# One transformer layer on one core: squares ahead of the last x tile, a held load, a third bank for A0b, the gate's row sum in two fp32r parts, and seventeen steps moved by a few matmuls

## The chip, the cores and the metric

The kernel runs on one core of a Trainium2 chip. The metric is device time in microseconds of that core. Five engines have queues of their own: PE (matmuls), ACT and DVE (elementwise work), POOL (slower elementwise work, and some DMAs) and SP (DMAs). They meet only at semaphores.

## The reference

One layer over 512 tokens of width 1024, in fp32:

```python
hn = rms_norm(h, ln_mix); z = hn @ w_in          # q1 q2 k1 k2 va | qf kf vf fg | qc kc vc
... per-head rms_norm of q and k, times a gain
o_a = diff_attention(...)        # 4 heads: softmax(q1 k1) - lam * softmax(q2 k2), then a per-head norm
o_b = forgetting_attention(...)  # 6 heads, bias from the cumulative sum of log_sigmoid(fg)
o_c = chunk_attention(...)       # 6 heads
h = h + concat(o_a, o_b, o_c) @ w_out
h = h + conv_gated_mlp(rms_norm(h, ln_ffn), w_up, conv_w, conv_b, w_down)
h = h + (p @ w_ple_proj) * sigmoid(rms_norm(h, ln_ple) @ w_ple_gate)
```

## The kernel before

**Precision.** A product of two fp32 matrices is three fp32r matmuls: each factor is split into a rounded part (`_h`, an ACT cast) and the rest (`_l`, a DVE subtraction); high by high, low by high and high by low are accumulated in one PSUM bank. `Th`, `Tl` are the split activations, feature by token; `A_0_h`, `A1b_l`, `w_hi`, `w_lo` and the like are split weights. `A_0_r`, `A1b_r`, `w_raw` are the raw weights as they land.

**Units and slots.** The input projection has eight column groups: A0 and A1 (two halves of the heads of group A), B0 to B2, C0 to C2. A0 and A1 each have a second part, A0b and A1b, with their second queries and keys. Each group is done in four units, one for each 128 tokens t, of 24 matmuls. A unit is a slot: `first_products` is slots 0 to 3 (A0), A0b is 4 to 7, A1 8 to 11, A1b 12 to 15, B0 16 to 19, and so on; the output projection follows from slot 40. In the trace A0 and A1 read alike (`A_z`, `A_zn`), and so do heads.

**After a unit** its bank `z` is evacuated: ACT squares the query and key columns (`A0b_sq`), DVE sums them by head (`A0b_rs`, a reduce, then a tensor_scalar, called TS below), POOL raises the result to the power -1/2 (also `A0b_rs`), DVE multiplies (`A0b_zn`). When all four t are done, `feature_cols` transposes `zn` on PE into a bank (`A_q_p`, then `A_k_p`; four transposes each), ACT and DVE split them (`A_q_q`, `A_q_ql`, `A_k_k`, `kl`) and POOL moves halves (`A_q_q`, `A_k_k` on POOL). Then come scores (`A_s`, `A_0b_s` and `A_1b_s`: part b is the second softmax), softmax pieces on DVE and ACT (`A_e`, `A_st`), transposes of the probabilities (`A_pt`, `A_ptc`, split into `pth`, `ptl`, `ptc`) and products with V (`A_po`). For group B, `forget_cumsum` transposes the gate columns (`pf`), scans them on DVE (`fs`) and transposes the sums back (`pq`).

**Banks.** PSUM has eight: z (2), s (2), t (3) and o (1). `in_unit` gives the four A0b units a bank by the letters of `"tots"[t]`: t, o, t, s. The first products hold both z and both s banks, `z0`.

**Order.** PE's order is written by hand: `run` takes one projection matmul after the other (index j, 0 to 23 in a slot) and puts in the next piece of an attention step at (slot, j) of the table `T`, with at least 3 matmuls between two pieces. The other engines' orders are made by a scheduler that follows data and a priority, raised for steps in `EARLY`. The numbers `wA1b`, `wO6` and the like in `T` say how many of a weight's four low parts POOL makes instead of DVE (by DMA that accumulates, or by a subtraction). The MLP and the gate are ordered by a planner, `Task` by `Task`, from costs and engine lists.

**The gate at the end.** Eight column blocks of h are squared on ACT (`n_sq`), added up on POOL or DVE (`sums`), and `total` sums over the partitions with one fp32 matmul by a matrix of ones (`pst<-sums,onec`). From `pst` come the row scales; the gate products `pg` do not wait for them, the outputs `y` do.

Of the kernel before, what the change touches and what calls it, by code (L numbers as in the profile page):

```python
# [15 lines left out]
P = 128  # L16
D = 1024
S = 512
# [59 lines left out]
def kernel(ctx: ExitStack, tc: tile.TileContext, x, xt0, xt, pt_in, small, bias_c,  # L78
# [53 lines left out]
    dve.memset(nhalf, -0.5)  # L132
    onec = cp.tile([P, 1], F32, tag="onec", name="onec")
    dve.memset(onec, 1.0)
    epsc = cp.tile([P, 1], F32, tag="epsc", name="epsc")
    dve.memset(epsc, EPS)
    ident = cp.tile([P, P], F32, tag="ident", name="ident")
# [153 lines left out]
    def load_x(t):  # L291
        tc.keep_in_program_order(nc.sync.dma_start(out=h[:, t, :], in_=x[t * P : (t + 1) * P, :]))
# [21 lines left out]
    for b in range(2):  # L314
        for i in range(2):
            c = HALF[1 - i]
            tc.keep_in_program_order(nc.gpsimd.tensor_scalar(
                KL[b][i][c, :], onec[c, :].broadcast_to([HD, S]), 0.0, 1.0, ALU.mult, ALU.mult))

    DONE = set()  # L320
# [14 lines left out]
    def first_products():  # L335
        for k in range(KD):
            n = 3 * P + 6
            if k % 2 == 0:
                wh, wl = (pi.tile([P, 768 + ROOM], F32R, tag=f"w{q}", bufs=W[q], name=f"A0_{k // 2}_{q}") for q in ("hi", "lo"))
            a = slice((k % 2) * n, (k % 2 + 1) * n)  # L340
            th, tl = Th[k // 4][:, k % 4, :], Tl[k // 4][:, k % 4, :]
            g = h[:, 3, 0:1] if k == 0 else col(C_MIX, k)
            if k == 0:
                for c in (slice(0, H), slice(H, S)):
                    dve.tensor_scalar(th[:, c], XB[k][:, c], g, 1.0, ALU.mult, ALU.mult)
            elif k == 3:
                dve.tensor_scalar(th, XB[k], g, 1.0, ALU.mult, ALU.mult)
            else:
                act.activation(th, XB[k], AF.Copy, scale=g)
            act.copy(wh[:, a], WA[k])  # L350
            dve.tensor_tensor(out=wl[:, a], in0=WA[k], in1=f32(wh[:, a]), op=ALU.subtract)
            dve.scalar_tensor_tensor(tl, XB[k], g, f32(th), ALU.mult, ALU.subtract)
            for i, (ta, w) in enumerate(((Th, wh), (Th, wl), (Tl, wh))):
                for t in range(NT):
                    pe.matmul(z0[t][:, :n], tcol(ta, k, t), w[:, a], start=k == 0 and i == 0, stop=k == KD - 1 and i == 2)
            if k == 1:
                load_x(3)
        ws = [w() for w in first_b]
        for t in range(NT):
            stats(t)  # L360
        ev = [in_unit("A0", 0, 3 * P + 6, t, None, []) for t in range(NT)]

        rs = [ev[t][0](rest=False) for t in range(2)]
        for t in range(NT):
            ev[t][1](rs[t])
            if t < 2:
                rs.append(ev[t + 2][0](rest=False))
        for t in range(NT):
            ev[t][0](sums=False)
        return ws  # L370
# [54 lines left out]
                                       rs[:, 4:8].unsqueeze(2).broadcast_to([P, 4, HD]), ALU.mult, ALU.mult)  # L425

    def feature_cols(zn, j, name):
        pt = bank("t", f"{name}_p")
        for t in range(NT):
            pe.transpose(pt[:, t * P : (t + 1) * P], zn[:, t, j * P : (j + 1) * P], ident)  # L430
        return pt
# [92 lines left out]
    def forget_cumsum():  # L524
# [199 lines left out]
    pairs = ["A0", "A1", "B0", "B1", "B2", "C0", "C1", "C2"]  # L724
    steps = {}

    def at(slot, gen, *args, start=1, early=0):
        steps.setdefault(slot, []).append((start, early, gen, args))

    def step(early, g):  # L730
        if early:
# [4 lines left out]

    def run(fill, todo):

        todo = [(start, early, gen(*args)) for start, early, gen, args in todo]
        after = 0  # L740
        for j in range(3 * KD):
            next(fill, None)
            while todo and j >= max(todo[0][0], after):
                try:
                    step(*todo[0][1:])
                    after = j + 3
# [5 lines left out]
        for _, early, g in todo:  # L752
# [6 lines left out]
    T = {  # L759
# [13 lines left out]
    }  # L773
    EARLY = {
# [6 lines left out]
    }  # L781

    def add(key, gen, *args):
        at(T[key][0], gen, *args, start=T[key][1], early=EARLY.get(key, 0))

    def lo_by(key, n):

# [3 lines left out]
    add("A0a", qk_cols, "A0", 0)  # L791
    add("A0b", qk_cols, "A0", 1)
    add("fc", forget_cumsum)
    add("A1a", qk_cols, "A1", 0)
    add("A1b", qk_cols, "A1", 1)
    for pr in ("A0", "A1"):
# [69 lines left out]
    slot = 0  # L866
    slot = 4
    act.pinned = dve.pinned = True
    ws_b = first_products()
    act.pinned = dve.pinned = False  # L870
    first_done = act.last, dve.last
    lam_init()
    def load_next(f, nxt, j):
        if j > 1:
            nxt.append(f())
# [51 lines left out]
    def mtmp(dt, m, name):  # L927
        return mp.tile([P, S * m], dt, tag="conv", bufs=CONV, name=name)
# [3 lines left out]
    def square(j):  # L932
        sq = mtmp(F32, 1, f"sq{j}")
        act.activation(sq, hj(j), AF.Square)
        return sq

    def total(tag, sums):

        pst = bank(tag, "pst")
        pe.matmul(pst, onec.broadcast_to([P, P]), sums, start=True, stop=True)  # L940
        return pst

    def roots(pst, rb, mt, sq):
# [468 lines left out]

    def first_load():
        q = loads.pop(0)
        q.do()
        q.end = 0.0

    def first_split(f, i, later=False):
# [215 lines left out]
        square3(j)  # L1634
    pst_slot, root_slots = Slot("t"), [Slot("conv"), Slot("conv")]

    def sums3():
# [200 lines left out]
```

## Time and profile before

| what | value |
|---|---|
| median of 3 runs | 689.13 us (688.67 to 690.82) |
| profiled execution: time, span | 689.12 us, 687.2 us |
| instructions | 12200 |
| busy PE, DVE, ACT, POOL | 98%, 81%, 61%, 33% of the span |
| mean granted PE clock | 0.998 |
| moved by DMA | 134.63 MB, mean 196 GB/s |

The page's share of busy time is over the whole span. The attention part reaches to about 303 us, the MLP to about 638, the gate to the end.

### The profile page before, as it was taken

The page shows a single profiled execution, that of the slowest core. Times are in us where ns is not written, and L with a number is a line of the kernel's source. Part 1 is how long each engine was busy: PE and PEld are TensorE (multiplying, and loading weights), DVE is VectorE, ACT ScalarE, POOL GpSimd, SP SyncE. Part 2 cuts the span into 40 slices and gives each one's busy share as a digit, 9 for nine tenths or more (in the row PEclk, how much of TensorE's full clock was granted, in tenths as well). Part 3 has the DMA queues.
Part 4 walks back from the last instruction along what each step waited for, and adds up shares of the span by engine and source line. Part 5 has one row for each costly group of instructions (what it writes and reads, how often), then busy time and mean ns, then how long its engine had stood idle before and what let it go on. Part 6 is the DMA issues. An engine that isn't in the chain of part 4 may idle for free.

```text
span 687.2 us, 12200 instructions
## 1 busy us (share of the span) xinstructions
PE 676.3 (98%) x4244; PEld 618.7 (90%) x4244; DVE 558.3 (81%) x1166; ACT 417.8 (61%) x811; POOL 227.9 (33%) x340
## 2 busy tenths in 40 slices
PE   9999999999999999999999999999999999999997
PEld 8988989998999988878889899999998898999886
DVE  7677787988878875789888897799888889888863
ACT  7657876776757653565576645556554566556821
POOL 6576765766564530421212111212111200000210
PEclk9999999999999999999999999999999999999999
DMA  9565679856655264389999899999999985462441
GB/s 329 200 169 115 193 239 275 235 172 213 228 136 186 87 220 139 122 203 244 164 271 219 170 263 234 268 219 203 223 287 259 176 217 155 145 229 95 153 123 61
DMA packets 57400, 134.63 MB, mean 196 GB/s; under 512 B 6486, under 2 KB 8150, under 8 KB 57340
## 3 DMA queue, kind: packets, MB, share of 16 engines
q1 hardware_dynamic: 45660, 107.60, 47.6%
q0 software_dynamic: 11392, 25.96, 23.1%
q8 instruction: 33, 0.54, 0.3%
q10 hardware_dynamic: 288, 0.31, 0.1%
q14 instruction: 27, 0.22, 0.1%
HBM read 125.83 MB, written 44.05 MB: 247 GB/s over the span
## 4 chain that ended last, share of the span: by engine, by line
PE 86%; DVE 4%; DMA 4%; ACT 2%; POOL 2%; issue 1%; SPq 0%; ACTq 0%; POOLq 0%; DVEq 0%
PE u L104 22%; PE dn_X L104 9%; PE C_z L104 6%; PE pg L104 6%; PE wo L104 6%; PE B_z L104 5%; PE sX L104 5%; PE dn_Y L104 4%; PE sY L104 3%; PE sZ L104 3%; PE dn_Z L104 2%; PE A1b_z L104 2%; PE pp L104 2%; DMA h<-in_x_dram 1%; PE B_s L104 1%; PE C_s L104 1%
## 5 line engine op out<-in xcount | busy, mean ns | idle before, releaser
L104 DVE TENSOR_TENSOR w_lo<-w_raw,w_hi 128x768 fp32r<-128x768 f32 (+5 forms) x154 | 115.0, 787 | 9.0 <-ACT w_hi L104 8.8
L104 ACT CAST w_hi<-w_raw 128x768 fp32r<-128x768 f32 (+5 forms) x154 | 99.6, 688 | 36.6 <-PE dn_X L104 7.1
L104 PE MATMUL u<-Th,w_hi 128*128 128x512 f32 x224 | 87.0, 391 | 0.0
L104 PE MATMUL u<-Tl,w_hi 128*128 128x512 f32 x224 | 86.9, 390 | 0.0
L104 PE MATMUL u<-Th,w_lo 128*128 128x512 f32 x224 | 86.8, 390 | 0.0
L104 PEld LDWEIGHTS u<-Th,w_lo 128*128 128x128 f32 x224 | 42.1, 188 | 9.0
L104 PEld LDWEIGHTS u<-Th,w_hi 128*128 128x128 f32 x224 | 42.0, 188 | 8.6 <-ACT Th L104 0.4
L104 PEld LDWEIGHTS u<-Tl,w_hi 128*128 128x128 f32 x224 | 42.1, 188 | 8.0
L104 DVE SCALAR_TENSOR_TENSOR c<-u,cols,c 128x511 f32<-128x511 f32 (+1 forms) x56 | 41.0, 746 | 6.2 <-ACT c L104 5.7
L104 POOL DMA_DIRECT2D usum<-usum x16 | 13.0, 812 | 91.5 <-DMA usum<-in_w_up_dram 56.9
L104 PE MATMUL dn_X<-g_ah,w_hi 128*128 128x256 f32 x144 | 39.8, 276 | 0.0
L104 PE MATMUL dn_X<-g_ah,w_lo 128*128 128x256 f32 x144 | 39.8, 276 | 0.0
L104 PE MATMUL dn_X<-g_al,w_hi 128*128 128x256 f32 x144 | 39.8, 276 | 0.0
L104 PE MATMUL B_z<-B_h,Th 128*128 128x384 f32 x96 | 33.5, 349 | 0.2 <-DVE A_st L104 0.2
L104 PE MATMUL C_z<-C_h,Th 128*128 128x384 f32 x96 | 33.5, 349 | 0.0
L104 PE MATMUL B_z<-B_l,Th 128*128 128x384 f32 x96 | 32.8, 342 | 0.0
L104 PE MATMUL B_z<-B_h,Tl 128*128 128x384 f32 x96 | 32.8, 342 | 0.0
L104 PE MATMUL C_z<-C_h,Tl 128*128 128x384 f32 x96 | 32.7, 341 | 0.0
L104 PE MATMUL C_z<-C_l,Th 128*128 128x384 f32 x96 | 32.5, 339 | 0.0
L104 ACT ACTIVATE c<-u,cols 128x512 f32<-128x512 f32 x28 | 21.5, 775 | 16.0 <-PE u L104 14.6
L104 POOL DMA_DIRECT2D dsum<-dsum x16 | 13.0, 813 | 51.8 <-DMA dsum<-dsum 22.2
L104 POOL TENSOR_TENSOR sums<-sums,n_sq 128x512 f32<-128x512 f32 x3 | 3.9, 1291 | 78.7 <-ACT n_sq L104 78.6
(501 smaller groups left out, 2381.5 us busy)
## 6 DMA issues: line engine op xcount, KB each, us to landing
w_raw<-in_w_up_dram SPq DMA_DIRECT2D x44, 384.0 KB, 7.0
dsum<-in_w_dsum_dram SPq DMA_DIRECT2D x12, 768.0 KB, 8.5
w_raw<-dsum SPq DMA_DIRECT2D x24, 384.0 KB, 5.9
usum<-in_w_usum_dram SPq DMA_DIRECT2D x32, 256.0 KB, 5.9
w_raw<-in_w_down_dram SPq DMA_DIRECT2D x18, 384.0 KB, 6.0
w_raw<-usum SPq DMA_DIRECT2D x16, 384.0 KB, 7.1
B_r<-in_w_in_dram SPq DMA_DIRECT2D x12, 384.0 KB, 3.8
C_r<-in_w_in_dram SPq DMA_DIRECT2D x12, 384.0 KB, 5.2
```

The lines of the kernel that those rows point to most:

```text
L104: ins = getattr(self.eng, op)(*a, **k)
```

## The change

It has seven parts.

1. **First products.** The square sum of the last x tile, `stats(3)`, stands behind the squares of the first two A0 units on ACT. `lam_init` is held behind a DVE instruction of k = 4. Two of the four `kl` fills go from POOL to DVE, and a ones column `oner` in fp32r is made on DVE.
2. **Banks.** A0b's unit t = 3 takes a t bank in place of an s bank; the transposes of A0's first queries and keys take s banks in place of t banks.
3. **`forget_cumsum` is cut in two.** The transposes back (`pq`) are a step of their own, `fq`, at (12, 0).
4. **`T`, `EARLY`, gaps.** Seventeen steps start one to ten matmuls earlier or later (`A0b` eight later, `A0n` ten later). `A1s12` has pieces 2 matmuls apart. The evacuations of seven units get a priority of their own, `A0b` gets 80, `A0n` and `A1b` lose theirs.
5. **Low parts.** A1b's fourth low part is a DVE subtraction and no longer an ACT copy and an accumulating POOL DMA; one more low part of the output weights is made on POOL.
6. **A held load.** The `w_up` load of 384 KB that SP issued at 14.57 us is issued behind SP's last instruction at that place of the program, among the loads near 280 us.
7. **The gate's sum.** `sums` is split into `sums_h` (an ACT cast) and `sums_l` (a DVE subtraction), and two fp32r matmuls take the place of the fp32 one. The planner's list has a task more there and orders some squares, splits and adds anew.

```diff
     def first_products():
...
+            if k == 4:
+                mid.append(dve.last)
...
-        for t in range(NT):
+        for t in range(3):
             stats(t)
         ev = [in_unit("A0", 0, 3 * P + 6, t, None, []) for t in range(NT)]
 
         rs = [ev[t][0](rest=False) for t in range(2)]
+        for t in range(3, NT):
+            stats(t)
...
-        pt = bank("t", f"{name}_p")
+        pt = bank("s" if name in ("A0_q0", "A0_k0") else "t", f"{name}_p")
...
-        evac()
+        with ahead(f"e{slot}"):
+            evac()
...
-            z = bank("tots"[t] if pr == "A0" else "z", f"{name}_z{t}")
+            z = bank("tott"[t] if pr == "A0" else "z", f"{name}_z{t}")
...
+        X["fs"] = fs
         yield
+
+    def forget_cols():
+        fs = X["fs"]
         pq = bank("t", "pq")
...
-        "A0a": (7, 8), "A0b": (9, 13), "fc": (11, 5), ...
+        "A0a": (7, 9), "A0b": (9, 21), "fc": (11, 3), ...
...
-        "wA1a": (0, 0), "wA1b": (1, 0), ... "wO6": (0, 1),
+        "wA1a": (0, 0), "wA1b": (0, 0), ... "wO6": (0, 2), "fq": (12, 0),
...
+    def two_parts(sums):
+
+        hi, lo = (mtmp(F32R, 1, f"sums_{q}") for q in "hl")
+        act.copy(hi, sums)
+        dve.tensor_tensor(out=lo, in0=sums, in1=f32(hi), op=ALU.subtract)
+        return hi, lo
...
+    def total_of_parts(tag, hi, lo):
+
+        pst = bank(tag, "pst")
+        pe.matmul(pst, oner.broadcast_to([P, P]), hi, start=True, stop=False)
+        pe.matmul(pst, oner.broadcast_to([P, P]), lo, start=False, stop=True)
         return pst
...
     def first_load():
         q = loads.pop(0)
-        q.do()
+        with tc.issue_after(sp.last):
+            q.do()
...
     def sums3():
-        v3["pst"] = total("t", v3["sums"])
+        v3["pst"] = total_of_parts("t", *v3["parts"])
...
     def at_sums():
-        p = pe_task(8, sums3, (), [v3["last"]], [pst_slot], [sum_slot])
+        slots = [Slot("conv"), Slot("conv")]
+        a = Task("do", [AC(S), DV(S)], parts3, [v3["last"]], slots, [sum_slot])
+        p = pe_task(4, sums3, (), [a], [pst_slot], slots)
```

PE's order around A0b's query and key transposes, first before and then changed (`A_z_625` and `A_z_627` are the same unit of A1, `A_z_693` the next):

```order
L104 MATMUL A_z_625<-A_2_l,Th_65 128x384
L104 MATMUL A_q_p<-ident,A0b_zn 128x128 x4
L104 MATMUL A_z_625<-A_2_h,Tl_67 128x384
L104 MATMUL A_z_625<-A_2_h,Th_65 128x384
L104 MATMUL A_z_625<-A_2_l,Th_65 128x384
L104 MATMUL A_k_p<-ident,A0b_zn 128x128 x4
```

```order
L104 MATMUL A_z_627<-A_3_h,Th_65 128x384
L104 MATMUL A_q_p<-ident,A0b_zn 128x128 x4
L104 MATMUL A_z_627<-A_3_l,Th_65 128x384
L104 MATMUL A_z_627<-A_3_h,Tl_67 128x384
L104 MATMUL A_k_p<-ident,A0b_zn 128x128 x4
L104 MATMUL A_z_693<-A_0_h,Th_64 128x384
```

Eight projection matmuls that stood behind the first group of transposes stand ahead of it; the scores that come later keep their place.

DVE's order from the low parts of A1b to A0b's last `zn`, before and changed (the tiles `A0b_rs_572` and `A0b_rs_574` are those of t = 3):

```order
L104 TENSOR_REDUCE A0b_rs_572<-A0b_sq_570 128x4
L104 TENSOR_TENSOR A1b_l<-A1b_r,A1b_h 128x512 x3
L104 TENSOR_SCALAR A0b_rs_572<-A0b_rs_572,rstd 128x4
L104 SCALAR_TENSOR_TENSOR A_V<-A_z_585,rstd,A_V 128x128
L104 TENSOR_REDUCE A_rs_614<-A_sq_612 128x4
L104 SCALAR_TENSOR_TENSOR A0b_zn<-A0b_z_519,A0b_rs_572 128x256
```

```order
L104 TENSOR_TENSOR A1b_l<-A1b_r,A1b_h 128x512
L104 TENSOR_SCALAR A0b_rs_510<-A0b_rs_510,rstd 128x4
L104 TENSOR_TENSOR A1b_l<-A1b_r,A1b_h 128x512
L104 TENSOR_REDUCE A0b_rs_574<-A0b_sq_572 128x4
L104 TENSOR_TENSOR A1b_l<-A1b_r,A1b_h 128x512 x2
L104 SCALAR_TENSOR_TENSOR A_V<-A_z_587,rstd,A_V 128x128
L104 TENSOR_SCALAR A0b_rs_574<-A0b_rs_574,rstd 128x4
L104 SCALAR_TENSOR_TENSOR A0b_zn<-A0b_z_483,A0b_rs_510 128x256
L104 TENSOR_REDUCE A_rs_616<-A_sq_614 128x4
L104 SCALAR_TENSOR_TENSOR A0b_zn<-A0b_z_521,A0b_rs_574 128x256
```

There are four subtractions in place of three ahead of the TS of t = 3, the TS of t = 2 is there too, and A_V comes ahead of the last TS.

DVE's order at the gate's sum, changed (before, the four adds were followed at once by the `wg_al` rows):

```order
L104 SCALAR_TENSOR_TENSOR xl<-w_raw_3897,cols,xh 128x512
L104 TENSOR_TENSOR sums_7364<-sums_7364,n_sq_7591 128x512
L104 TENSOR_TENSOR sums_7364<-sums_7364,n_sq_7630 128x512
L104 TENSOR_TENSOR sums_7364<-sums_7364,n_sq_7633 128x512
L104 TENSOR_TENSOR sums_7364<-sums_7364,n_sq_7636 128x512
L104 TENSOR_TENSOR sums_l<-sums_7364,sums_h 128x512
L104 SCALAR_TENSOR_TENSOR wg_al<-w_raw_3899,cols,wg_ah 128x512
```

A subtraction that waits for ACT's cast of the finished sum has come in between.

More of the change, by code (lines that the diff above doesn't have):

```diff
@@ L134 @@
     dve.memset(onec, 1.0)
+    oner = cp.tile([P, 1], F32R, tag="oner", name="oner")
+    dve.tensor_scalar(oner, onec, 1.0, 1.0, ALU.mult, ALU.mult)
     epsc = cp.tile([P, 1], F32, tag="epsc", name="epsc")
@@ L316 @@
             c = HALF[1 - i]
-            tc.keep_in_program_order(nc.gpsimd.tensor_scalar(
+            tc.keep_in_program_order((nc.vector if b else nc.gpsimd).tensor_scalar(
                 KL[b][i][c, :], onec[c, :].broadcast_to([HD, S]), 0.0, 1.0, ALU.mult, ALU.mult))
@@ L725, with at, ahead @@
     steps = {}
-    def at(slot, gen, *args, start=1, early=0):
-        steps.setdefault(slot, []).append((start, early, gen, args))
+    def at(slot, gen, *args, start=1, early=0, gap=3):
+        steps.setdefault(slot, []).append((start, early, gap, gen, args))
+    def ahead(key):
+        return tc.high_priority(offset=EARLY[key]) if EARLY.get(key) else ExitStack()
     def step(early, g):
@@ L737, in run @@
     def run(fill, todo):
-        todo = [(start, early, gen(*args)) for start, early, gen, args in todo]
+        todo = [(start, early, gap, gen(*args)) for start, early, gap, gen, args in todo]
         after = 0
@@ L744, in run @@
                 try:
-                    step(*todo[0][1:])
-                    after = j + 3
+                    _, early, gap, g = todo[0]
+                    step(early, g)
+                    after = j + gap
                     break
@@ L751, in run @@
             pass
-        for _, early, g in todo:
+        for _, early, _, g in todo:
             try:
@@ L759 @@
     T = {
[4 rows of a table removed]
[4 rows of a table added]
         "B0s0": (24, 2), "B0s1": (24, 5), "B0p0": (25, 2), "B0v0": (25, 8), "B0p1": (26, 2), "B0v1": (26, 8),
[5 rows of a table removed]
[5 rows of a table added]
         "C2s1": (42, 1), "C2p0": (42, 6), "C2v0": (43, 23), "C2p1": (44, 3), "C2v1": (46, 5), "wA0b": (4, 2),
[2 rows of a table removed]
[2 rows of a table added]
     }
     EARLY = {
[6 rows of a table removed]
[6 rows of a table added]
     }
+    GAP = {k[4:]: v for k, v in EARLY.items() if k.startswith("gap_")}
     def add(key, gen, *args):
-        at(T[key][0], gen, *args, start=T[key][1], early=EARLY.get(key, 0))
+        at(T[key][0], gen, *args, start=T[key][1], early=EARLY.get(key, 0), gap=GAP.get(key, 3))
     def lo_by(key, n):
@@ L793 @@
     add("fc", forget_cumsum)
+    add("fq", forget_cols)
     add("A1a", qk_cols, "A1", 0)
@@ L868 @@
     act.pinned = dve.pinned = True
+    mid = []
     ws_b = first_products()
@@ L871 @@
     first_done = act.last, dve.last
-    lam_init()
+    with tc.issue_after(mid[0]):
+        lam_init()
     def load_next(f, nxt, j):
@@ L940, in total @@
         pe.matmul(pst, onec.broadcast_to([P, P]), sums, start=True, stop=True)
+        return pst
+    def total_of_parts(tag, hi, lo):
+        pst = bank(tag, "pst")
+        pe.matmul(pst, oner.broadcast_to([P, P]), hi, start=True, stop=False)
+        pe.matmul(pst, oner.broadcast_to([P, P]), lo, start=False, stop=True)
         return pst
@@ L1635, with parts3 @@
     pst_slot, root_slots = Slot("t"), [Slot("conv"), Slot("conv")]
+    def parts3():
+        v3["parts"] = two_parts(v3["sums"])
     def sums3():
-        v3["pst"] = total("t", v3["sums"])
+        v3["pst"] = total_of_parts("t", *v3["parts"])
     def roots3():
```

34 rows, old and new, of tables (EARLY, T) are left out of this document.

## The prediction

> **What bounds the kernel.** I read the page's first part, then PE's busy time by stage, then PE's waits, then each wait in the timeline.
>
> ```profile
> PE 676.3 (98%) x4244; PEld 618.7 (90%) x4244; DVE 558.3 (81%) x1166; ACT 417.8 (61%) x811; POOL 227.9 (33%) x340
> 22.00:44.00 22.00, 19.43 (x149) 19.00 (x148) 17.27 (x46) 15.24 (x32) 16.70 (x25) 1.00 0.44 147
> 44.00:62.00 18.00, 16.45 (x100) 15.10 (x101) 13.73 (x42) 13.09 (x30) 13.02 (x22) 1.00 0.36 91
> 100.00:160.00 60.00, 59.51 (x363) 56.06 (x362) 51.39 (x182) 46.23 (x110) 38.32 (x59) 1.00 0.68 203
> 160.00:235.00 75.00, 74.80 (x463) 71.61 (x462) 60.17 (x181) 51.11 (x126) 44.81 (x72) 1.00 0.56 175
> 235.00:638.00 403.00, 403.00 (x2602) 364.78 (x2601) 337.95 (x550) 230.38 (x396) 71.71 (x87) 1.00 0.80 206
> PE A_s L104 <- DVE A_st L104: 1.5, 4, 0.6
> PE A_q_p L104 <- DVE A0b_zn L104: 1.3, 1, 1.3
> PE A0b_z L104 <- DVE oall L104: 1.3, 1, 1.3
> PE pq L104 <- DVE fs L104: 0.8, 1, 0.8
> ```
>
> PE is busy for 676.3 of 687.2 us, so 10.9 us of idle time is all that better order can win, and the clock is granted in full (1.00). From 235 to 638 us PE never stops. Its waits lie in the attention part: 2.57 us idle from 22 to 44, 1.55 from 44 to 62. The waits list names them; three are places that the change touches (A0b_z, A_q_p, pq), 3.4 us together. The question is whether these waits go, or only move. The sum is made against the profiled execution, 689.12 us (span 687.2 and 1.9 around it), which is the median of the runs (689.13).
>
> **A0b's bank and transposes.**
>
> ```profile
> 30.17 0.28 PE L104 MATMUL A0b_z<-A0b_l,Th 128*128 128x256 f32 x1
> 30.28 0.28 PE L104 MATMUL A0b_z<-A0b_h,Tl 128*128 128x256 f32 x1
> 31.81 0.36 PE L104 MATMUL A0b_z<-A0b_h,Th 128*128 128x256 f32 x1 [1.25 <-DVE oall L104]
> 30.41 0.34 DVE L104 SCALAR_TENSOR_TENSOR A_V<-A_z,rstd,A_V 128x128 fp32r<-128x128 f32 x1
> 39.38 1.14 ACT L104 CAST A1b_h<-A1b_r 128x512 fp32r<-128x512 f32 x2
> 39.65 2.09 DVE L104 TENSOR_TENSOR A1b_l<-A1b_r,A1b_h 128x512 fp32r<-128x512 f32 x3
> 41.37 0.98 POOL L175 DMA_DIRECT2D A1b_l<-A1b_r  x1 [1.37 <-ACT A1b_l L104]
> 41.66 0.36 DVE L104 TENSOR_SCALAR A0b_rs<-A0b_rs,rstd 128x4 f32<-128x4 f32 x1
> 42.41 1.02 POOL L104 TENSOR_TENSOR A0b_rs<-A0b_rs,nhalf 128x4 f32<-128x4 f32 x1
> 43.47 0.42 DVE L104 SCALAR_TENSOR_TENSOR A0b_zn<-A0b_z,A0b_rs 128x256 f32<-128x256 f32 x1 [0.47 <-POOL A0b_rs L104]
> 43.95 0.33 PE L104 MATMUL A_q_p<-ident,A0b_zn 128*128 128x128 f32 x1 [1.32 <-DVE A0b_zn L104]
> 54.68 1.57 PE A_z L104 x9
> ```
>
> At 30.28 A0b's fourth unit waits for DVE to read the s bank of an A0 unit. A t bank is free there, so PE goes on: 31.81 - 30.28, less a pitch of 0.11 (30.28 - 30.17), is 1.42 us won at that place. The new waiter on s banks is the transposes of A0's queries; by my count of DVE's new queue the last reader ends about 31.3 and they come about 31.5, so 0 to 0.3 is lost there; I take 0.
>
> But PE's next wait is not for a bank. A0b_zn of t = 3 ends a DVE queue that runs from 30.41 to 41.66 (11.25 us) without waiting for PE. The new order has one A1b_l more in it (2.09/3, or 0.67 by starts) and one TS more (about 0.1), and starts about 0.4 earlier, because the squares ahead of the last x tile let A0's sums begin sooner: its last TS starts about 42.05 instead of 41.66. POOL, on the other side, no longer stands behind the A1b_l DMA (41.37 to 42.35), which had held its power to 42.41. So the power comes at 42.35 to 42.45 as before, zn near 43.4, and the last transpose at 43.85 to 44.0. PE, 1.42 early, fills this time with the eight projection matmuls that are now ahead of the step (8 x 1.57/9 = 1.39) and then waits as long as it did. What is won is eight matmuls done ahead.
>
> ```profile
> 48.87 0.61 POOL L104 TENSOR_SCALAR A_k_k<-A_k_k 64x512 fp32r<-64x512 f32 x1
> 49.68 0.28 PE L104 MATMUL A_0b_s<-A_k_k,A_q_q 128*128 128x256 f32 x1
> ```
>
> They are not kept either. The first scores of part b read the last A_k_k move, which ends at 49.48, 5.5 us of ACT, DVE and POOL work after the transposes. PE came at 49.68, just behind it. Now it comes at 49.68 - 1.39 = 48.3, the move 0 to 0.2 earlier than before (the key transposes follow one matmul sooner): a new wait of about 1.1 us, and 0.25 of the 1.42 is left. Bounds: -0.1, if zn is later, and 1.4, if the whole chain is earlier. I take 0.25, since every row of this chain has a fixed predecessor here. The softmax waits that follow (A_s on A_st) are DVE's own chain, which starts with these scores; 0.3 is carried to 54 us.
>
> **pq.**
>
> ```profile
> 56.72 1.22 DVE L104 TENSOR_TENSOR_SCAN fs<-onec,pf 128x512 f32<-128x512 f32 x1 [0.36 <-PE pf L104]
> 56.88 0.33 PE L104 MATMUL A_z<-A_h,Tl 128*128 128x384 f32 x1
> 58.00 0.66 PE L104 MATMUL pq<-ident,fs 128*128 128x128 f32 x4 [0.79 <-DVE fs L104]
> 60.58 1.10 DVE L104 SCALAR_TENSOR_TENSOR A_e<-A_e,A_st,A_3b_e 128x512 f32<-128x512 f32 x1 [0.59 <-POOL A_3b_e L104]
> 62.53 0.60 PE L104 MATMUL A_pt<-ident,A_e 128*128 128x128 f32 x4
> 65.29 1.00 PE L104 MATMUL A_po<-ptc,A_V 128*128 128x256 f32 x4
> 97.65 0.50 PE L104 MATMUL A_s<-A_k_k,A_q_q 128*128 128x512 f32 x1 [0.55 <-DVE A_st L104]
> ```
>
> The transposes back move behind 15 more matmuls, over 2 us; the scan of 1.22 is hidden, and 58.00 - 56.88 - 0.17 = 0.95 goes. PE would be 1.25 early at A_pt (62.53). What is late next: A_e, which ends at 61.68 and comes perhaps 0.3 sooner, lets PE keep about 1.1. Then ptc: DVE has a reduce of A1b ahead of it now and ACT a square, so PE's last A_po products, which waited a little at 65.29, start about 65.0 to 65.1. Here 0.6 is left (0.3 to 1.1). Up to 100 us `A0n` ten matmuls later takes a short wait away, but the scores at 97.65 wait for A_st, at the end of DVE's chain, and hold PE again: 0.6.
>
> **The other steps** move by one to three matmuls, 0.2 to 0.5 us, some later and some earlier, in stages where PE idles for 0.49 of 60 us and 0.20 of 75. That is all they can win; what a step put too early can lose is its own shift. I take 0, with -0.5 to +0.7 as bounds.
>
> **The load, the low parts, the fills.**
>
> ```profile
> w_raw<-in_w_up_dram SPq DMA_DIRECT2D x44, 384.0 KB, 7.0
> 296.83 0.84 ACT L104 CAST w_hi<-w_raw 128x768 fp32r<-128x768 f32 x1
> 278.27 1.29 POOL L182 TENSOR_TENSOR wo_l<-wo_r,wo_h 128x512 fp32r<-128x512 f32 x1 [18.92 <-PE wo L104]
> ```
>
> The held load, till now behind the x loads, is issued near 280 and lands some 7 us later, 9 us ahead of its cast: 0. On SP one weight load stands behind it, which is needed later still. Behind the old place the loads of A0's and A1b's weights can only come sooner, and their casts aren't on the path. The two fills on DVE come ahead of the first x, which DVE has to wait for anyway. The extra low part on POOL, 1.29 us from 278 on, ends near 280, and PE's last output products, which read it, come later: 0.
>
> **The gate.**
>
> ```profile
> 639.97 6.18 PE pg L104 x27
> 646.15 0.86 PE pst L104 x2
> L104 DVE SCALAR_TENSOR_TENSOR w_lo<-w_raw,cols,w_hi x2: 740/1245/1750, 638.5 to 640.2; 128x512 fp32r<-128x512 f32 x2
> 637.08 2.67 POOL L104 TENSOR_TENSOR sums<-sums,n_sq 128x512 f32<-128x512 f32 x2 [6.32 <-ACT n_sq L104]
> 642.74 3.07 DVE L104 TENSOR_TENSOR sums<-sums,n_sq 128x512 f32<-128x512 f32 x4
> ```
>
> The chain of waits gives the fp32 sum 0.86, and a pg matmul of as many columns 6.18/27 = 0.23. Two fp32r matmuls are 0.46, so 0.40 is won, if the parts are there. They are a cast (about 0.6, by the two of A1b_h above) and a subtraction (about 0.7, by A1b_l) behind the last add, which ended at 642.74 + 3.07 = 645.81, hardly ahead of PE at 646.15. If the add stays there, `sums_l` is ready at 647.1 to 647.2 and PE, which wants it at 646.15 + 0.23 = 646.4, waits 0.8: the gate loses 0.4. But one thing is gone in the new order. In the old one the third POOL add runs to 639.75, and the w_lo that DVE starts at 638.5 takes 1750 ns in place of 740: it ends 0.54 after POOL does. A square moved up in ACT's queue lets POOL end near 638.3; DVE is then 1.0 sooner, its last add ends near 644.8, `sums_l` near 646.2, and by these rows PE need not wait; for what two semaphores cost I take 0.1 and a gain of 0.3 (bounds -0.4 and 0.4).
>
> The Trainium skill ("SBUF — State Buffer", section "SBUF: two separate sides") says that VectorE and GpSimd share a port pair under an exclusive lock, taken by a VectorE instruction with two SBUF inputs against a GpSimd one that reads SBUF, and held to its end. The 1750 ns row agrees. By that rule the gate gains 0.3; were the long w_lo something else, the sum would be 0.7 higher, at 688.9. The rows give both figures without it.
>
> **Sum:** 689.12 - 0.6 (attention) - 0.3 (gate) = 688.2.
>
> **The rivals.**
>
> *A, the waits move (0.55).* This is the sum: 688.2. It is 687.2 with all 0.7 of the other steps and a little of the 1.4, and 689.5 if everything won is lost again and the steps lose 0.4 beside it.
>
> *B, the waits go (0.28).* It says that the DVE chain before A0b_zn is earlier too, by A0b's priority of 80 and those of its evacuations. For it: zn is held by queue order, not by data, and ACT and POOL have gaps of over 1 us there. Against it: the new order in DVE's queue, which is longer. Then 1.3 + 1.3 + 0.8 from the waits list and the 0.3 at the gate go: 685.4.
>
> *C, the parts are late (0.09).* The adds stay where they are and the gate loses 0.4: 688.9. For it: DVE's four adds keep their order.
>
> *D, slower (0.08).* A1b's fourth low part now stands in DVE's queue ahead of A0b's last TS.
>
> ```profile
> 33.61 3.76 DMA A1b_r<-in_w_in_dram
> ```
>
> If its raw weight lands late, TS, zn and PE wait for a DMA. ACT's last two casts ran without waiting at 39.38 and DVE's subtraction comes about 1 us behind, so that there is 1 us of slack; a delay beyond 1 us goes straight into PE, and from 3 us on the kernel is slower than 689.13 by more than 0.3%. At a delay of one landing (3.76) the time is 688.2 + 3.8 - 1 = 691.0 or, with no slack left, 692.0.
>
> **The numbers.** What a measurement can tell from no change is about 0.3%, 2.07 us: 687.06 and 691.20. A and C lie within it but for A's low end (0.04 of it goes below); B is below but for its weak form, in which half of the waits go (0.02). So faster 0.30, same 0.62, slower 0.08. The range takes in B's end and A's upper end with C's 0.7 on top: 685.3 to 690.2. It leaves out D and the little below B. A's own range is 687.2 to 689.5.
>
> **What would show it.** Right: no wait of A0b_z near 30; A_q_p's wait still 1.2 to 1.7; a new wait of some 1 us at A_0b_s near 49; none at pq; a longer one at A_s near 97; pst taking 0.45 to 0.6; the w_lo row near 740 ns. Wrong: a zn of t = 3 a microsecond sooner (then B), a pst wait of 0.8 (C), DVE waiting for A1b_h (D), or stalls in the MLP, where the row from 235 to 638 has none.

## The result, and the profile after

The changed kernel takes 700.86 us (median of 6 runs, 700.39 to 701.18) against 689.24 for the kernel before (6 runs): a ratio of 1.0161, 95% interval 1.0144 to 1.0177. It is 11.6 us slower; the forecast was 688.2. The profiled execution took 701.18 us with a span of 699.0.

First the page's busy row and PE's busy time by stage, after:

```profile
PE 690.7 (99%) x4244; PEld 627.7 (90%) x4244; DVE 560.1 (80%) x1170; ACT 417.0 (60%) x811; POOL 228.3 (33%) x338
22.00:44.00 22.00, 21.76 (x160) 21.48 (x159) 18.15 (x47) 13.87 (x32) 15.88 (x22) 1.00 0.48 154
44.00:62.00 18.00, 16.79 (x107) 15.16 (x105) 14.37 (x44) 14.25 (x33) 13.64 (x23) 1.00 0.21 55
235.00:638.00 403.00, 403.00 (x2500) 360.47 (x2499) 326.87 (x533) 221.95 (x381) 72.02 (x87) 1.00 0.79 203
```

The attention stages did what they should: from 22 to 44 us PE is idle for 0.24 us in place of 2.57. But the row from 235 to 638 shows PE as busy as before, for 403.00 of 403.00 us at a granted clock of 1.00, and holds 2500 matmuls in place of 2602. PE did not wait; each matmul took longer.

PE's waits after:

```profile
PE A_s L104 <- DVE A_st L104: 1.3, 3, 0.7
PE A_z L104 <- DVE A_zn L104: 0.4, 1, 0.4
PE A_0b_s L104 <- POOL A_k_k L104: 0.3, 1, 0.3
PE A_q_p L104 <- DVE A0b_zn L104: 0.2, 1, 0.2
PE A_po L104 <- DVE ptc L104: 0.2, 1, 0.2
```

Those of A0b_z (1.3) and pq (0.8) are gone, that of A_q_p fell from 1.3 to 0.2. PE's idle time fell from 10.9 to 8.3 us and its busy time rose from 676.3 to 690.7: less idle time than before, and a longer span.

Where the time went is seen when the same matmuls are laid side by side. Three places of PE's timeline, first of the kernel before:

```profile
60.60 0.28 PE L104 MATMUL A1b_z<-A1b_h,Th 128*128 128x256 f32 x1
296.63 1.02 PE L104 MATMUL pst<-sums,onec 128*128 128x512 f32 x2
645.99 1.02 PE L104 MATMUL pst<-sums,onec 128*128 128x512 f32 x2
```

and after (the first unit of A1b, the MLP's row sum, the gate's row sum):

```profile
58.38 0.28 PE L104 MATMUL A1b_z<-A1b_h,Th 128*128 128x256 f32 x1
296.56 1.02 PE L104 MATMUL pst<-sums,onec 128*128 128x512 f32 x2
657.63 0.39 PE L104 MATMUL pst<-sums_h,oner 128*128 128x512 f32 x1
```

PE is 2.22 us ahead at 60 us, level at 296, and 11.64 behind at the gate. Between these the offset grows evenly: by all matched matmuls it is -0.93 at 260 us, +1.09 at 346, +4.6 at 449, +9.1 at 583 and +11.8 at 661. A wait would be a step in this curve; an even slope means that every matmul takes longer.

Two groups of PE in the MLP (count; busy time in us, mean ns), before and then after:

```profile
L104 PE MATMUL u<-Th,w_hi 128*128 128x512 f32 x224 | 87.0, 391 | 0.0
L104 PE MATMUL dn_X<-g_ah,w_hi 128*128 128x256 f32 x144 | 39.8, 276 | 0.0
```

```profile
L104 PE MATMUL u<-Th,w_hi 128*128 128x512 f32 x224 | 88.1, 395 | 0.0
L104 PE MATMUL dn_X<-g_ah,w_hi 128*128 128x256 f32 x144 | 40.5, 281 | 0.0
```

Same counts, 4 to 5 ns more each. Matmuls overlap (the 391 ns of an up product stand beside starts 227.5 ns apart), so what counts is the time from start to start: an up product (`u`) of 512 columns takes 227.5 ns before and 233.2 after, a down product (`dn_X`) of 256 columns 113.5 and 118.7. Of a matmul's two operands one, the stationary, is loaded by an instruction of its own (PEld in the busy row); the other is called the moving one. In the built programs 996 products of 512 columns and 1596 of 256 have split weights as their stationary operand: 2592 x 5 ns = 13.0 us, close to the 12.7 by which the offset grew.

No diff line touches these matmuls. What moved is where their operands lie. `oner`, one fp32 number per partition, takes 32 bytes in the pool of small tiles, and the pool of split weights, which follows, starts at byte 59040 of each partition in place of 59008 (addresses are those in the built programs). `Th` and `Tl` (24704 on) and `g_ah`, `g_al` stay where they were.

### The profile page after: what moved, and what is told of

It is laid out like the page before. It is cut to its first block, busy times and chain, and to the rows that moved or that the text cites. A ratio compares the mean times of both kernels' runs of the same rounds, so it can differ in the third digit from the quotient of the medians.

```text
span 699.0 us, 12209 instructions
## 1 busy us (share of the span) xinstructions
PE 690.7 (99%) x4244; PEld 627.7 (90%) x4244; DVE 560.1 (80%) x1170; ACT 417.0 (60%) x811; POOL 228.3 (33%) x338
## 4 chain that ended last, share of the span: by engine, by line
PE 84%; DVE 6%; DMA 4%; POOL 2%; ACT 2%; issue 1%; POOLq 0%; DVEq 0%; ACTq 0%
PE u L104 22%; PE dn_X L104 9%; PE wo L104 6%; PE pg L104 6%; PE C_z L104 6%; PE sX L104 5%; PE dn_Y L104 4%; PE B_z L104 4%; PE sY L104 3%; PE sZ L104 3%; PE dn_Z L104 2%; PE pp L104 2%; PE A1b_z L104 2%; PE C_po L104 1%; PE C_s L104 1%; DMA h<-in_x_dram 1%
## 5 line engine op out<-in xcount | busy, mean ns | idle before, releaser
L104 POOL DMA_DIRECT2D dsum<-in_w_dadd_dram x16 | 13.6, 853 | 50.5 <-DMA dsum<-in_w_dadd_dram 21.8
```

The source lines that it names most:

```text
L104: ins = getattr(self.eng, op)(*a, **k)
```

## The experiments

Each compares with runs of the kernel before on the same chip. Only e7, e12, e13 and e14 also change the order of queues, and their text says where; in the others only places differ.

**Places in steps of 32 and 64 bytes.** The first four runs move the weights, or the attention's own tiles.

In e1, the changed kernel with the weights at 59072:

```diff
-    oner = cp.tile([P, 1], F32R, tag="oner", name="oner")
+    oner = cp.tile([P, 16], F32R, tag="oner", name="oner")[:, 0:1]
```

> The changed kernel with one number altered: oner takes 64 bytes in place of 32, so that every weight tile that lies behind it begins at a multiple of 64 again, as before the change. The order of no engine's queue changes. Theory 1 (place): the 32 bytes of oner moved all weight tiles to 32 beyond a multiple of 64, and a matmul that reads such a tile costs 5 to 7 ns more; between 258 and 660 us the changed kernel fell 12.9 us behind (from 1.1 ahead to 11.8 behind), so the time should be 700.9 - 12.9 = 688.0, between 687 and 689. Rival 1 (order): the new order, with fewer waits on PE, lets PE fall into a slower cadence: 700 to 701, as the change. Rival 2 (the gate's or the held load's traffic slows PE): 700 to 701 too.

Measured: 700.88 us, ratio 1.0176 (1.0159 to 1.0193). The multiple of 64 fell. The rivals order and traffic forecast the same time, so that this run alone cannot tell places from them.

In e2 and e3, the kernel *before* with the weights 32 and 64 bytes further:

```diff
-    gq = cp.tile([P, 8], F32, tag="gq", name="gq")
+    gq = cp.tile([P, 16], F32, tag="gq", name="gq")[:, 0:8]     # e2
+    gq = cp.tile([P, 24], F32, tag="gq", name="gq")[:, 0:8]     # e3
```

> The kernel before, where only the tile gq, the last ahead of the weight pool, is 32 bytes longer; nothing else of the change. Theory 1 (place): all weight tiles begin 32 beyond a multiple of 64, and the MLP and the output projection run at 233 ns for 512 columns and 119 for 256 in place of 227 and 113: 689.2 + 12 to 14 = 701 to 703. Rivals 1 and 2 (order, traffic): 689.2, no change.

> The control: the kernel before with gq 64 bytes longer. Theory 1 (multiples of 64): 689.2, no change. If any move of the weight tiles changes the time (another rule than 64), or if 128 matters, it differs from 689.2 by more than 1 us. Rivals 1 and 2: 689.2.

Measured: 702.96 us (ratio 1.0195, 1.0179 to 1.0212) and 702.88 (1.0197, 1.018 to 1.0215). e2 is the decisive run here: with not one of the change's steps, 32 bytes of empty space cost 13.6 us, so order and traffic are not needed for the loss. In PE's stage row of e2 the count is that of the changed kernel within two:

```profile
235.00:638.00 403.00, 403.00 (x2498) 360.38 (x2497) 327.39 (x534) 221.65 (x381) 69.50 (x85) 1.00 0.78 202
```

In e4 the attention's tiles go to multiples of 64 beside e1 (`fgb`, `rs`, `fa` and `otmp` a few columns longer).

> The kernel of e1_after_space with four small attention tiles lengthened, so that the tiles of V, of the probabilities and their split parts and of the normed queries and keys, which begin 32 beyond a multiple of 64 in both kernels, begin at multiples of 64 too. Theory 1 (place, for every operand): the attention part's matmuls, of which about six in ten run at the slow cadence in both kernels, lose 3 to 6 ns each on some 500 to 1000 matmuls: 1 to 4 us less than e1_after_space, 684 to 687. If only weight tiles matter, or these matmuls wait for other engines: as e1_after_space. Rivals 1 and 2: as the change.

Measured: 700.74 us (1.0167, 1.0152 to 1.0181), nothing gained over e1.

**Is it the multiple of 128?** The old start, 59008, is one; 59040 and 59072 are not. So e5 puts the weights of the changed kernel at 59136, e6 the attention's tiles at multiples of 128 beside it, e7 takes the gate's parts back in e5, and e8 moves `Th` and `Tl` of the kernel before by 64. (In e8 the weights moved too, by 128; its expectation says only that they stay at multiples of 128.)

```diff
-    gq = cp.tile([P, 8], F32, tag="gq", name="gq")
+    gq = cp.tile([P, 32], F32, tag="gq", name="gq")[:, 0:8]     # e5
```

```diff
+    space = cp.tile([P, 16], F32, tag="space", name="space")    # e8, ahead of Th
-    nhalf = cp.tile([P, 8], F32, tag="nhalf", name="nhalf")
+    nhalf = cp.tile([P, 24], F32, tag="nhalf", name="nhalf")[:, 0:8]
```

> The changed kernel, with the small tile gq lengthened so that the pool of split weights starts at a multiple of 128 bytes again (59136), as it did before the change (59008); no queue's order is touched. Theory (PE reads the stationary operand of a 512-column matmul at 227 ns only if it starts at a multiple of 128 bytes, else at 233): the cadence in the MLP goes back to 226 to 227 ns and the 12.9 us lost between 258 and 660 us come back: 700.9 - 12.9 = 688.0, with 686.5 to 688.5 as bounds; that is also what the prediction's sum said of the steps alone (688.2). Rival (a particular address counts, such as the old start 59008 or its distance to another tile, not the multiple of 128): 700.9, cadence still 233. Rival (the cadence is slow from the moved steps and not from places): 700.9.

> As the run with the weights at a multiple of 128, and besides the attention's own tiles (q, k, kl, V, the split probabilities, zn, the exponentials, the bias) all start at multiples of 128 bytes; in both kernels of the change they start 64 or 96 bytes off. Theory (the same rule holds for every stationary operand): about half of the attention part's 512- and 256-column matmuls on these tiles lose 6 ns each; by some 500 to 800 such matmuls 1.5 to 5 us, so 683 to 686.5, less where the attention waits for other engines instead. Rival (only the weights' stationary tiles in the MLP count, or the attention has slack elsewhere): as the other run, 688.0.

> The changed kernel with the weights at a multiple of 128, and the gate's sum back as one fp32 matmul, with the planner's task and order of before there. It measures the gate's part alone. The prediction's step says that two fp32r parts gain 0.3 us (bounds -0.4 and 0.4): this run would be 688.3 against 688.0 for the run with both parts. Rival C of the prediction (parts late): 687.6.

> The kernel before with Th and Tl, the split activations, moved by 64 bytes and the weights left at multiples of 128. In the MLP's up products and the output products Th and Tl are the moving operand, in the input projection the stationary one. Theory (the stationary operand alone counts): the input projection's matmuls (slots up to 40, about 22 to 235 us, 384 and 256 columns, some 930) become 5 to 6 ns slower, so 689.2 + 4 to 5 = 693 to 694, and the MLP keeps 227 ns. Rival (either operand counts): the up products, some 1800, slow down too, 689.2 + 5 + 11 = 705. Rival (the moving operand alone counts, or the weights' own place): 700 or 689.2.

Measured: e5 699.63 us (1.0155, 1.0141 to 1.0169), e6 699.82 (1.0153, 1.0139 to 1.0167), e7 699.43 (1.0146, 1.0132 to 1.016), e8 700.95 (1.017, 1.0156 to 1.0184). The 128-byte theory fell with e5, and with it e6's hope; of e8's sums only that of the moving operand alone (700) came near, which e5, where that operand hadn't moved, contradicts. e7 and e5 differ by less than their scatter. But the traces now held many pairs of places. Sorted by the distance from the moving rows' start to the stationary's start, modulo 256 bytes, nearly all the fast 512-column products of the output projection, the MLP and the gate were those at 0, and the fast 256-column products those at 64. In the changed kernel's gate, where the weights `wg_ah` lie elsewhere, products of 512 columns at distance 0 go at the fast rate even there.

**The distance, modulo 256.** Three runs test it. e9 is the changed kernel with `oner` in the unused bytes of `epsc`, so that every tile is back at its old place:

```diff
-    oner = cp.tile([P, 1], F32R, tag="oner", name="oner")
-    epsc = cp.tile([P, 1], F32, tag="epsc", name="epsc")
+    both = cp.tile([P, 2], F32R, tag="epsc", name="epsc")
+    oner, epsc = both[:, 1:2], f32(both[:, 0:1])
```

e10 makes `gq` 64 columns long (weights at 59264, 256 beyond the old place); e11 is the kernel before with only the `space` tile of e8, which moves `Th`, `Tl` and the weights together by 64 and leaves `g_ah`, `g_al` where they are.

> The changed kernel with oner and epsc in one tile, so that oner takes no 32 bytes of its own and every tile stands at the address it has in the kernel before (weights from 59008); no queue's order is touched. The run with the weights 128 bytes further kept the slow cadence, so it isn't the multiple of 128 that counts. New theory (the cadence depends on the distance, modulo 256 bytes, between where a matmul's moving rows start and where the next stationary starts: 0 is fast for 512 columns, 64 for 256; these are the distances in the kernel before): the cadence is back at 227 and 113 ns in the MLP, and the time is 700.9 less the 12.9 lost there: 688.0 (687 to 688.5). Rival (the moved steps have a part in the slow cadence): over 692.

> The changed kernel with gq lengthened so that the weights start at 59264, which is 256 bytes beyond the place they have in the kernel before; no order touched. Theory (distance modulo 256): as fast as with the old addresses, 688.0. Rival (a modulus of 512 or more, or the address itself): slow, 700.

> The kernel before with Th, Tl and the weights all moved by 64 bytes; the tiles of the down products' moving operand (g_ah, g_al) stay. Theory (the distance counts): the up products (512 columns, distance still 0) and the sums sX, sY, sZ (256 columns, distance still 64) keep 227 and 113 ns; the down products (distance 64 becomes 128), 912 of 256 columns, take 118 to 119 ns: 912 x 5.3 = 4.8 us more, and some 200 gate products with the weights stationary up to 6 ns more: 689.2 + 5 to 6 = 694 to 695. Rival (the stationary operand's own address counts): up products and sums become slow too, 701 to 703, as when the weights alone moved by 64.

Measured: e9 688.95 us (ratio 0.9994, 0.9985 to 1.0002), e10 689.01 (0.9989, 0.9979 to 0.9998), e11 696.8 (1.0103, 1.0088 to 1.0118). e9 and e10 have the old rate, and the count of before within two (e9 first):

```profile
235.00:638.00 403.00, 403.00 (x2600) 364.61 (x2600) 337.47 (x548) 230.07 (x395) 74.33 (x89) 1.00 0.80 206
235.00:638.00 403.00, 403.00 (x2601) 364.70 (x2600) 337.65 (x548) 230.35 (x396) 73.84 (x89) 1.00 0.79 206
```

In e9 the offset to the kernel before is -0.82 us at every matched matmul from 380 to 637 us. e11 separates the distance from the address: all its weights lie where e3 has them, and yet in its groups the up products are fast and the down products slow:

```profile
L104 PE MATMUL u<-Th,w_hi 128*128 128x512 f32 x224 | 86.8, 390 | 0.0
L104 PE MATMUL dn_X<-g_ah,w_hi 128*128 128x256 f32 x144 | 40.5, 281 | 0.0
```

In e3 both were slow. The address rival wanted 701 to 703 for e11 and falls. The distance theory's own 694 to 695 was some 2 us short, and the reason can be read from the same trace: the forecast let all sums keep their distance of 64, but only those whose moving rows are `Th`, `Tl` do. The 384 sums whose moving rows are `xh`, `xl`, tiles that did not move, come to 128 and take 118.8 ns in place of 113.5, which is 2.0 us. Here the same kind of weights has two rates in one kernel:

```profile
L104 PE MATMUL sZ<-xh,w_hi 128*128 128x256 f32 x32 | 9.0, 281 | 0.0
L104 PE MATMUL sZ<-Th,w_hi 128*128 128x256 f32 x32 | 8.8, 276 | 0.0
```

The table has the mean from start to start, with the distance that it belongs to (steps in which PE waited, and the few sums at another distance, are left out):

| kernel | u, 512 columns: distance, ns | dn_X, 256: distance, ns | sums by Th, Tl, 256: distance, ns | sums by xh, xl, 256: distance, ns |
|---|---|---|---|---|
| before | 0, 227.5 | 64, 113.5 | 64, 113.5 | 64, 113.5 |
| after, e2 | 32, 233.2 | 96, 118.7 | 96, 118.7 | 96, 118.7 |
| e1, e3 | 64, 233.2 | 128, 118.7 | 128, 118.6 | 128, 118.6 |
| e5 | 128, 232.8 | 192, 117.8 | 192, 117.8 | 192, 117.7 |
| e8 | 64, 233.2 | 192, 117.2 | 128, 118.7 | 192, 117.8 |
| e9 | 0, 227.6 | 64, 113.5 | 64, 113.5 | 64, 113.4 |
| e10 | 0, 227.5 | 64, 113.5 | 64, 113.5 | 64, 113.5 |
| e11 | 0, 227.4 | 128, 118.7 | 64, 114.2 | 128, 118.8 |

One place does not fit. The last gate products have `wg_ah`, `wg_al` as weights, and their operands lie at the same addresses in e8 and in e11, at a distance of 192. Yet from start to start those of 256 columns take 113.3 ns in e8, the fast rate, and 117.8 in e11:

```profile
L104 PE MATMUL pg<-Th,wg_ah 128*128 128x256 f32 x16 | 4.4, 276 | 0.0
L104 PE MATMUL pg<-Th,wg_ah 128*128 128x256 f32 x16 | 4.5, 279 | 0.0
```

Those of 512 columns take 229.2 and 229.1, between the two rates. From 235 us on the distance sorts all other groups of ten steps or more into the two rates; at 192 something beside it has a part, and what that is stays open.

**The gate at the fast rate.** e12 is e9 with the fp32 sum back:

```diff
-        v3["pst"] = total_of_parts("t", *v3["parts"])
+        v3["pst"] = total("t", v3["sums"])
...
-        slots = [Slot("conv"), Slot("conv")]
-        a = Task("do", [AC(S), DV(S)], parts3, [v3["last"]], slots, [sum_slot])
-        p = pe_task(4, sums3, (), [a], [pst_slot], slots)
+        p = pe_task(8, sums3, (), [v3["last"]], [pst_slot], [sum_slot])
```

> The changed kernel with all tiles at their old addresses, and the gate's sum as one fp32 matmul, in the planner's order of before. It isolates the gate's part at the fast cadence. The prediction's step (two parts gain 0.3, bounds -0.4 and 0.4): 688.3 against 688.0 for both parts. Rival C of the prediction (the parts are late and the gate loses 0.4): 687.6. At the slow cadence the same pair was 699.43 against 699.63.

Measured: 687.86 us, ratio 0.998 (0.997 to 0.999). The mean of its 10 runs is 0.9 us below that of e9's 12 on the same chip (95% interval 0.2 to 1.6), so the two parts cost time. By its interval e12 is also a little faster than the kernel before; that of e9 reaches 1.0002.

**Two things left open.** e13 gives seven column groups of e12 a distance of their own, to look for the fast one of 384 columns; e14 is e12 with A0b's part undone.

```diff
-        c0 = NEAR if n == 2 * P else 0
+        c0 = NEAR if n == 2 * P else BY_GROUP.get(name[:2], 0) if n == 3 * P else 0    # e13
```

```diff
-        pt = bank("s" if name in ("A0_q0", "A0_k0") else "t", f"{name}_p")
+        pt = bank("t", f"{name}_p")
-            z = bank("tott"[t] if pr == "A0" else "z", f"{name}_z{t}")
+            z = bank("tots"[t] if pr == "A0" else "z", f"{name}_z{t}")
-        "A0b": (9, 21)
+        "A0b": (9, 13)                 # and A0b's priority of 80 gone: e14
```

> The changed kernel with the old places and the gate's one fp32 matmul, and the split weights of seven column groups each shifted within their tiles, so that the distance modulo 256 from the moving rows (weights) to the next stationary (Th, Tl) is, for 384 columns, 64 (A1), 224 (B0), 192 (B1), 160 (B2), 128 (C0), 96 (C1), 32 (C2) in place of 0; no order touched. Read from the trace by group. Known so far, over 384 columns' pure 160 ns: 14.6 ns at 0, 14.5 at 224, 13.6 at 192, 15.8 at 128. Theory (a fast distance exists for each shape, as 0 for 512 and 64 for 256 columns): one of 32, 64, 96, 160 gives 10 to 11 ns, with its neighbours slow; 32 if the fast distance falls evenly with the columns. Rival (384 columns have no fast distance, the attention's elementwise work disturbs them anyway): all stay at 13 to 16. The time: within 1 us of 687.9 in either case, as most groups only change from one slow distance to another.

> The changed kernel with the old places and the gate's one fp32 matmul, and A0b's part undone: bank letters t, o, t, s, all feature transposes in t banks, step A0b at (9, 13) without its priority. The prediction's step: A0b's wait of 1.3 near 30 and the later wait at A_q_p come back and the scores' wait goes, worth 0.25 to 0.3 us in all: 688.2 against 687.9. Rival B of the prediction (the waits went for good): 1.4 or more slower, 689.3. Rival (the part is worth nothing): 687.9.

Measured: e13 687.99 us (0.9981, 0.9968 to 0.9993). From start to start, with steps over 190 ns left out, the 384 columns take 174.4 ns at a distance of 64, 173.7 at 224, 173.9 at 192, 176.1 at 160, 176.0 at 128, 175.2 at 96, 174.0 at 32, and 174.3 to 175.2 at 0 (e12): no step like the 5 ns of the other shapes. No multiple of 32 is a fast distance for 384 columns here, and the theory's forecast of one fell.

e14: 688.75 us (0.9983, 0.9974 to 0.9991), beside e12's 0.998. By the means against e13 of the same chip, which has other distances for its 384 columns besides, A0b's part is worth 0.5 us (-0.3 to 1.3): its sign is not settled, and the prediction's 0.25 to 0.3 lies within. The waits show the part's mechanism, though, e14 without it and then e12 with it:

```profile
PE A0b_z L104 <- DVE A0b_rs L104: 1.6, 1, 1.6
PE A_q_p L104 <- DVE A0b_zn L104: 1.5, 2, 0.9
```

```profile
PE A_q_p L104 <- DVE A0b_zn L104: 1.1, 2, 0.9
PE A_z L104 <- DVE A_zn L104: 0.4, 1, 0.4
PE A_0b_s L104 <- POOL A_k_k L104: 0.3, 1, 0.3
```

Without the part the bank's wait is back at 1.6. With it that wait is gone, the transposes still wait 1.1, and two waits that e14 lacks, 0.4 and 0.3, stand behind them: the wait moves, and part of it is saved.

## Why the prediction was wrong

**The step that failed** is the sum's premise that PE's busy time stays as it is: "PE is busy for 676.3 of 687.2 us, so 10.9 us of idle time is all that better order can win". From there on only waits were costed. The small additions got no time ("The two fills on DVE come ahead of the first x"), and beside them `oner` was costed nowhere. It was looked at as an instruction, and it is one of no weight; as a tile it moved every split weight by 32 bytes. The sum had no term for places, and the range none either: all of the 0.08 given to a slower kernel went to rival D, a late load at 691 to 692, and that did not come: between 30 and 45 us DVE waits for POOL alone in the changed kernel (1.0 and 0.4 us). What the runs showed in place of zero: 13.6 us for the same 32 bytes without the change (e2), and 11.9 between the changed kernel with and without them (700.86 and 688.95; 11.5 by their ratios to the kernel before).

It could have been seen. The row from 235 to 638 was quoted for having no idle time, and the only loss looked for there was a wait. With PE busy throughout, whatever changes the rate of its 2602 matmuls counts in full, and the kernel before has a hint in its own lines (`load_w`, with a cut):

```python
    ROOM, NARROW, NEAR = 64, 16, 48
...
        c0 = NEAR if n == 2 * P else 0
```

Split weights for 256 columns are put 48 columns (`NEAR`) or, in another function, 16 (`NARROW`) into tiles that have 64 to spare. These numbers do nothing for the data. 16 columns are 64 bytes, which for stationary weights is a distance of 64; 48 columns are 192 bytes, which for A0b's weights, the moving operand there, is 64 as well. An offset that the arithmetic does not need may be there for the timing.

**What the prediction said would show it** could not tell: "stalls in the MLP" was to be the sign of a wrong forecast there, and there were none.

**The rest of the sum,** at the old places. The forecast for all steps was 688.2, 0.9 below its base; e9 is 0.4 below the kernel before by the ratio (1.0 below to 0.1 above). By parts:

- *A0b's bank*: right that the wait near 30 goes; PE's timeline after runs through there without one. Right also that the wait moves, and about right in sum. In e9 the transposes wait 0.46 + 0.89 = 1.35 (forecast 1.2 to 1.7):

```profile
42.77 0.33 PE L104 MATMUL A_q_p<-ident,A0b_zn 128*128 128x128 f32 x1 [0.46 <-DVE A0b_zn L104]
43.99 0.33 PE L104 MATMUL A_q_p<-ident,A0b_zn 128*128 128x128 f32 x1 [0.89 <-DVE A0b_zn L104]
45.50 0.41 PE L104 MATMUL A_z<-A_h,Th 128*128 128x384 f32 x1 [0.40 <-DVE A_zn L104]
49.45 0.39 PE L104 MATMUL A_0b_s<-A_k_k,A_q_q 128*128 128x256 f32 x1 [0.32 <-POOL A_k_k L104]
```

  The last zn starts the transposes at 43.99 (forecast 43.85 to 44.0, before 43.95), so rival B fell. The first scores wait 0.32 and not 1.1, because a bank wait of 0.40 that was not in the sum stands ahead of them. In all, the lead over the kernel before grows from 22 to 54 us by 0.1 in e9's trace (0.24 to 0.33) and by 0.5 in e12's (-0.12 to 0.37); the forecast was 0.3.
- *pq*: right, no wait. In e9 PE is 1.28 ahead at A_pt (forecast 1.25), 1.03 behind the A_po products (forecast 0.6, 0.3 to 1.1) and 0.82 at the scores near 97 (forecast 0.6); 0.24 of each stands already at 22 us in this trace. A_s waits there 0.74 in the changed kernel in place of 0.55, as said.
- *The attention as a whole*: -0.82 in e9 against -0.6, and 1.4 us (0.7 to 2.1) by e12's ratio, which has all of it and the old gate.
- *The gate*: wrong sign. POOL's, DVE's and then PE's timelines of e9 there:

```profile
637.15 1.31 POOL L104 TENSOR_TENSOR sums<-sums,n_sq 128x512 f32<-128x512 f32 x1 [4.26 <-ACT n_sq L104]
638.17 1.49 DVE L104 SCALAR_TENSOR_TENSOR w_lo<-w_raw,cols,w_hi 128x512 fp32r<-128x512 f32 x2 [0.30 <-ACT w_hi L104]
641.45 3.06 DVE L104 TENSOR_TENSOR sums<-sums,n_sq 128x512 f32<-128x512 f32 x4
645.20 0.69 DVE L104 TENSOR_TENSOR sums_l<-sums,sums_h 128x512 fp32r<-128x512 f32 x1 [0.69 <-ACT sums_h L104]
```

```profile
644.88 0.39 PE L104 MATMUL pg<-Tl,w_hi 128*128 128x512 f32 x1
645.23 0.50 PE L104 MATMUL pst<-sums_h,epsc 128*128 128x512 f32 x1
645.95 0.50 PE L104 MATMUL pst<-sums_l,epsc 128*128 128x512 f32 x1 [0.23 <-DVE sums_l L104]
646.29 0.39 PE L104 MATMUL pg<-Th,w_hi 128*128 128x512 f32 x1
```

  (`epsc` is e9's name for the tile with the ones.) The chain came out as forecast: `w_lo` takes 742 and 830 ns and no longer 1750, the last add ends at 644.51 (forecast 644.8), `sums_l` at 645.89 (forecast 646.2). What failed is the other side. The step asked whether `sums_l` is there when PE "wants it at 646.15 + 0.23 = 646.4", which was PE's time of before; the sum's own 0.6 of attention gain, 0.82 in fact, brings PE there at 645.6, ahead of `sums_l`. From the end of the last `pg` slot, 644.88 + 0.23 = 645.11, to the next `pg` at 646.29 are 1.18 us, where the fp32 sum took 0.86: 0.3 lost in place of 0.3 won, by this one trace. Rival C had the sign and nearly the size (0.4), but not the way: it held that the adds stay where they were, and they start 1.3 us sooner (641.45 for 642.74). In the changed kernel itself PE came 12 us late, both parts were there, and they took 658.29 - 657.63 = 0.66, 0.2 less than the fp32 sum; only there do they pay:

```profile
657.63 0.39 PE L104 MATMUL pst<-sums_h,oner 128*128 128x512 f32 x1
657.95 0.50 PE L104 MATMUL pst<-sums_l,oner 128*128 128x512 f32 x1
658.29 0.40 PE L104 MATMUL pg<-Th,w_hi 128*128 128x512 f32 x1
```

The Trainium skill's rule on the port pair of VectorE and GpSimd ("SBUF — State Buffer", section "SBUF: two separate sides") agrees with the short `w_lo`: in e9 it starts 0.29 us before POOL's add ends, takes 830 ns, and ends 0.54 after that add, as the one of 1750 ns did in the kernel before.

## What to carry to other kernels

Where PE is busy throughout, compare how many matmuls a stage holds, not only its idle time: 2500 for 2602 at the same busy time and clock says that the rate fell, where the matmuls are the same. Before a new tile is put into a pool, however small, see which tiles stand behind it; and when a time moves by per cents with no wait to show for it, put the old addresses back first, with every instruction of the change kept. When a step is forecast to bring PE sooner somewhere, the later steps have to be worked out with PE that much sooner.

## What the runs showed of the hardware that was not expected

In these runs the rate of fp32r matmuls goes with the distance between moving and stationary operand, modulo 256 bytes within a partition. For 512 columns a distance of 0 gives 227.4 to 227.6 ns from start to start, and 32, 64 and 128 give 232.8 to 233.2. For 256 columns 64 gives 113.4 to 114.2, and 96, 128 and 192 give 117.2 to 118.8. The gate products at 192 are the exception: 113.3 in e8 and 117.8 in e11 for 256 columns, with the same addresses, and 229 for 512. For 384 columns none of the eight multiples of 32 stands out (173.7 to 176.1). No address alone decides: a shift of the weights by 256 bytes costs nothing (e10), the same place of the weights has both rates (e11), and so has the same place of `Th` (before and e5). The granted clock reads 1.00 in both cases, and so does PE's busy share. Why these distances are the fast ones no run shows; a collision of the reads of the stationary operand with those of the moving one would fit, but it is only argued.
